# Moving the output transposes and second outputs to other places in the tensor engine's written order

## The chip, the cores and the metric

One NeuronCore of one Trainium2 chip runs the whole program. The metric is the device time of one execution in microseconds (us), lower is better. The kernel before was timed three times: 1958.93, 1961.59 and 1966.63 us, median 1961.59.

## The reference, cut to what matters

One layer of a hybrid encoder is applied to a prompt of 1024 tokens and a sample of 512, both 1024 channels wide: RMSNorm, one projection into eleven blocks of 1024 columns, a bidirectional gated linear recurrence (8 heads of 128) beside a gated short convolution, two branch projections merged by sigmoid gates, an output projection, a residual and a last RMSNorm. What the change touches is the recurrence of one head:

```python
def one_direction(f_raw, lb, reverse):
    logf, one_minus_f = _forget(f_raw, lb)
    ...
    return _gla_chunk_scan(qh, kh, vh, logf)
o = one_direction(f_fw, lb_fw, False) + one_direction(f_bw, lb_bw, True)
o = o * lax.rsqrt(jnp.mean(o * o, axis=-1, keepdims=True) + EPS)
o = o * hnorm_g
...
p_a = jnp.einsum('ble,ed->bld', o_a * jax.nn.silu(z_a), w_a)
# in _gla_chunk_scan, per chunk
o = scores @ v + (q * exp(G)) @ S
S = S * exp(G_last) + k_dec^T @ v
```

## The kernel before, in words

The program has three stages. Up to about 905 us it normalizes the tokens and projects the prompt. From there to about 1519 us a loop runs the recurrence of all heads, with the sample's projections as filling between its small products. After it come the branch and output projections.

The loop makes 25 passes, here called turns (`i`, with `h, m = divmod(i, 3)`); three turns are a round, one for each head `h`. A turn prepares one block of 512 tokens (`cur`) and multiplies the block before it (`prev`). The blocks of a head are the two halves of the prompt (`groups[h]`, blocks 0 and 1) and the sample (`sample[h]`). In turn `m` = 0 `prev` is the sample of the head before, in turn 1 block 0 of this head, in turn 2 block 1.

TensorE (PE) runs in the order in which the source is written (`manual_schedule(engines={T.engine})`); the orders of the other engines and of the queue that issues transfers (SP) are chosen by a planner, which takes earlier written work first among what it holds ready. The pieces of a turn are:

- `near_scores` and `scores` (with `far_scores`): products of 32 and 64 columns (L451, L485), picked into `near` by VectorE (DVE, L464) and copied into `pt` by ScalarE (ACT, L475, L476, L487).
- `transpose_keys` (L500): 6 to 8 transposes of the decayed keys `K` into two PSUM buffers named "u", of which there are three, copied out by ACT (L502).
- `decays`: fourteen ACT copies (L435, L436) and fourteen DVE multiplications (L437, L438) that prepare `K`, `Q` and `cats` of `cur`, and GpSimd (POOL) products `T` (L425).
- `contributions` (L513): what `prev` adds to the states, in two "u" buffers, copied out by ACT (L514). When a group is complete, `states` (DVE, L522) runs the recurrence over chunks.
- `outputs(g, b)` (L537): a block's result in the only "o" buffer; ACT squares it with a sum (L541), DVE and POOL (L542, L81) make the reciprocal root, ACT scales it into `oz` (L545).
- `finish(g)`: four transposes of `oz` for each block in one "u" buffer (L551), a DVE multiplication by the gate `zg` (L552) that frees that buffer, and the store (L553). The prompt's gate `zgp` has one buffer and is loaded on the SP queue.
- `unit()`: one of the sample's projections, 24 products of 512 columns (L77; two of them have 96, L70), here called dense.

The order of PE in a round before, with | around dense units: turn 0: near, keys, outputs of block 0 | unit | scores, contributions | unit | outputs of block 1 | unit. Turn 1: near, keys | unit | scores, contributions | unit | outputs of the sample. Turn 2: near, keys | unit | `finish` of both prompt blocks, scores, `finish` of the sample, contributions | unit, unit. The results that are finished in round `h` are those of head `h - 1`, seven rounds in all; the last head is finished behind the loop.

Of the kernel before, what the change touches and what calls it, by code (L numbers as in the profile page):

```python
# [20 lines left out]
NH = 8  # L21
KT = 8
TB = 512
# [20 lines left out]
def trunk_kernel(ctx: ExitStack, tc: tile.TileContext, xs, w, outs, masks_d, ident_d):  # L44
    nc = tc.nc
    V, A, G, T = nc.vector, nc.scalar, nc.gpsimd, nc.tensor
    load = store = nc.sync.dma_start
# [31 lines left out]
    def rsqrt(pool, t, name):  # L79
        r = pool.tile(list(t.shape), F32, name=f"rs_{name}")  # L80
        G.tensor_tensor(r, t, neghalf[:, :t.shape[-1]], op=ALU.pow)  # L81
        return r
# [25 lines left out]
    zg_d = dram.tile([NH, P, 2 * TB], F32, name="zg_d")  # L108
# [40 lines left out]
    with ExitStack() as st:  # L149
# [178 lines left out]
        for j in range(NH):  # L328
# [7 lines left out]
            for t, pr in enumerate(project2("ff", "fb", j)):  # L336
                for d, z in zip((1, 0), pr):
                    f = cp.tile([P, TB], F32, name="sg", bufs=4)
                    k = cp.tile([P, TB], F32, name="sk", bufs=2)
# [39 lines left out]
    with outer:  # L379
# [7 lines left out]
        def gtile(name, shape, bufs=1):  # L387
            return gp.tile([P, *shape], F32, name=name, bufs=bufs)

        def bank(name, bufs, shape=(CPB, P)):  # L390
            return ps.tile([P, *shape], F32, name=name, bufs=bufs)
# [12 lines left out]
        def loaded(group, b):  # L404

            k = Block(group, b)
            src = fkq_d[k.tb][group.h]
            load(k.F, src[:, 0:2, :])
            load(k.K, src[:, 2:4, :])
            load(k.q, src[:, 4, :])  # L410
            return k

        def decays(k):

            F, K, q = k.F, k.K, k.q
            k.Q = Q = gtile("Q", [2, TB], 3)
            V.scalar_tensor_tensor(Q, ap(q, 0, [[0, 2], [1, TB]]), float(P) ** -0.5, F, op0=ALU.mult, op1=ALU.mult)
            k.kd = gtile("kd", [TB], 2)
            V.tensor_tensor(k.kd, K[:, 0, :], K[:, 1, :], op=ALU.add)

            Ts = [(F, TB)]
            while Ts[-1][1] > CPB:
                t, m = Ts[-1]
                tn = gtile(f"T{TB * 2 // m}", [2, m // 2], 1 if m // 2 > CPB else 4)
                G.tensor_tensor(tn, ap(t, 0, [[m, 2], [2, m // 2]]), ap(t, 1, [[m, 2], [2, m // 2]]), op=ALU.mult)  # L425
                Ts.append((tn, m // 2))
            k.total = Ts[-1][0]
            k.cats = []
            for hs, (t, m) in zip(LEVELS, Ts):
                nb = TB // (2 * hs)  # L430
                cat = gtile("cat", [2, TB], 8)
                k.cats.append(cat)
                kall = ap(K, TB, [[2 * hs, nb], [hs - TB, 2], [1, hs]])
                qall = ap(Q, 0, [[2 * hs, nb], [hs + TB, 2], [1, hs]])
                A.copy(ap(cat, 0, [[2 * hs, nb], [hs, 2], [1, hs]]), kall)  # L435
                A.copy(ap(cat, TB, [[2 * hs, nb], [hs, 2], [1, hs]]), qall)  # L436
                V.tensor_tensor(kall, kall, ap(t, m + 1, [[2, nb], [-m - 1, 2], [0, hs]]), op=ALU.mult)  # L437
                V.tensor_tensor(qall, qall, ap(t, 1, [[2, nb], [m - 1, 2], [0, hs]]), op=ALU.mult)  # L438
# [15 lines left out]
        def near_scores(k):  # L454

            k.sc = []
            score_products(k, range(4))
            k.near = near = gtile("near", [CPB, Q32])
            A.activation(near, k.sc[0][:, 0, :, :], AF.Copy, scale=float(P) ** -0.5)
            for li in range(1, 4):  # L460
                pick(k, li)
# [27 lines left out]
        def chunks_for(k, d):  # L489

            cs = [c for c in range(CPB) if (k.b * CPB + c < k.g.n - 1 if d else k.b * CPB + c > 0)]
            return cs, slice(cs[0], cs[-1] + 1)

        def transpose_keys(k):
            k.kT = []
            for d in (1, 0):
                cs, span = chunks_for(k, d)
                p = bank("u", 3)
                for c in cs:
                    T.transpose(p[:, c, :], k.K[:, d, c * P:(c + 1) * P], ident)  # L500
                kT = gtile("kT", [CPB, P], 2)
                A.copy(kT[:, span, :], p[:, span, :])  # L502
                k.kT.append(kT)

        def contributions(k):
            g = k.g
            if k.b == 0:
                g.us = gtile(f"us{g.n}", [2, g.n, P])
            for d, kT in zip((1, 0), k.kT):
                cs, span = chunks_for(k, d)  # L510
                p = bank("u", 3)
                for c in cs:
                    T.matmul(p[:, c, :], kT[:, c, :], g.v[:, k.b * CPB + c, :], start=True, stop=True)  # L513
                A.copy(g.us[:, d, k.b * CPB + span.start:k.b * CPB + span.stop, :], p[:, span, :])  # L514
            g.done.append(k)
# [9 lines left out]
        def outputs(g, b):  # L525
            for k in g.done[b:b + 1]:
                p = bank("o", 1)
                for c in range(CPB):
                    n = k.b * CPB + c
                    cols = slice(c * P, (c + 1) * P)  # L530
                    mms = [(k.pt[:, c, :], g.v[:, n, :])]
                    if n > 0:
                        mms.append((k.Q[:, 1, cols], g.us[:, 1, n - 1, :]))
                    if n < g.n - 1:
                        mms.append((k.Q[:, 0, cols], g.us[:, 0, n + 1, :]))
                    for m, (l, r) in enumerate(mms):
                        T.matmul(p[:, c, :], l, r, start=m == 0, stop=m == len(mms) - 1)  # L537
                k.oz = oz = gtile("oz", [CPB, P], 3)
                ss = gtile("sso", [CPB], 2)
                for c in range(CPB):  # L540
                    A.activation(oz[:, c, :], p[:, c, :], AF.Square, accum_out=ss[:, c:c + 1])  # L541
                V.tensor_scalar(ss, ss, 1.0 / P, EPS, op0=ALU.mult, op1=ALU.add)  # L542
                r = rsqrt(gp, ss, "o")
                for c in range(CPB):
                    A.activation(oz[:, c, :], p[:, c, :], AF.Copy, scale=r[:, c:c + 1])  # L545

        def finish(g):
            for k in g.done:
                p = bank("u", 3)
                for c in range(CPB):  # L550
                    T.transpose(p[:, c, :], k.oz[:, c, :], ident)  # L551
                V.tensor_tensor(k.oz, p, g.zg[:, k.b * TB:(k.b + 1) * TB].rearrange("p (c t) -> p c t", c=CPB), op=ALU.mult)  # L552
                store(oz_d[k.tb][g.h], k.oz.rearrange("p c t -> p (c t)"))  # L553
# [13 lines left out]
        sample = {}  # L567
# [74 lines left out]
        def prepare(n):  # L642
            while todo and len(ready) < n:
                p, m = todo.pop(0)
                ready.append((m, p()))

        def unit():
            prepare(AHEAD + 1)
            if ready:
                m, x = ready.pop(0)  # L650
                m(x)

        def prompt_group(h):
            return Group(h, (0, 1))
# [7 lines left out]
        groups = [prompt_group(h) for h in range(NH)]  # L662
# [6 lines left out]
        prev = None  # L669
        for i in range(len(order) + 1):  # L670
            h, m = divmod(i, 3)
            cur = None
            if i < len(order):
                cur = nxt if order[i][0] else sample[h]
                if i + 1 < len(order) and order[i + 1][0]:
                    nxt = loaded(*order[i + 1])
            if prev:
                near_scores(prev)
                transpose_keys(prev)
            if m == 0 and h:  # L680
                outputs(groups[h - 1], 0)
            if cur:
                decays(cur)
                if cur.b == 0:
                    values(cur.g)
            unit()
            if m == 2 and h:
                finish(groups[h - 1])
            if prev:
                scores(prev)  # L690
            if m == 2:
                if h:
                    finish(sample[h - 1].g)
                groups[h].zg = gtile("zgp", [2 * TB])
                load(groups[h].zg, zg_d[h])
            if prev:
                contributions(prev)
            unit()
            if m == 0 and h:
                outputs(groups[h - 1], 1)  # L700
            if m == 1 and h:
                outputs(sample[h - 1].g, 0)
            if m != 1:
                unit()
            if prev and len(prev.g.done) == len(prev.g.tbs):
                states(prev.g)
            prev = cur
        outputs(sample[NH - 1].g, 0)
        unit()
        finish(groups[NH - 1])  # L710
        finish(sample[NH - 1].g)
        left.close()
        right.close()

# [328 lines left out]
```

## Time and profile before

| | before |
|---|---|
| median of three runs | 1961.59 us |
| the profiled execution's own time | 1959.61 us |
| its span, first to last instruction | 1957.8 us |
| PE busy | 1918.9 us, 98% of the span |
| DVE busy | 1462.7 us, 75% |
| ACT busy | 941.5 us, 48% |
| mean granted clock of PE | 0.993 |

The profile is of one execution. Its own time is 1.8 us more than its span, and 2.0 us under the median. [...] A timeline row gives the start, the duration, engine, line, operation, out<-in, shape and count, and in brackets the idle time of the engine before it and who ended that. Matmuls are pipelined, so that rows overlap: the time that a piece takes is read from its start to the start of the next piece. All times are from the first instruction.

### The profile page before, as it was taken

The page shows a single profiled execution, that of the slowest core. Times are in us where ns is not written, and L with a number is a line of the kernel's source. Part 1 is how long each engine was busy: PE and PEld are TensorE (multiplying, and loading weights), DVE is VectorE, ACT ScalarE, POOL GpSimd, SP SyncE. Part 2 cuts the span into 40 slices and gives each one's busy share as a digit, 9 for nine tenths or more (in the row PEclk, how much of TensorE's full clock was granted, in tenths as well). Part 3 has the DMA queues.
Part 4 walks back from the last instruction along what each step waited for, and adds up shares of the span by engine and source line. Part 5 has one row for each costly group of instructions (what it writes and reads, how often), then busy time and mean ns, then how long its engine had stood idle before and what let it go on. Part 6 is the DMA issues. An engine that isn't in the chain of part 4 may idle for free.

```text
span 1957.8 us, 38000 instructions
## 1 busy us (share of the span) xinstructions
PE 1918.9 (98%) x14772; PEld 1619.0 (83%) x14772; DVE 1462.7 (75%) x2423; ACT 941.5 (48%) x1946; POOL 144.4 (7%) x220
## 2 busy tenths in 40 slices
PE   8999999999999999999989999999999999999998
PEld 8988888888888888887878888888888888888786
DVE  6558787878787878785776577777773547889996
ACT  6433434434444343434676576676674333434432
POOL 1000000000000000002221122121220000000000
PEclk8999999999999999999999999999999999999999
DMA  7466676676676767668755554554534866879852
GB/s 211 125 212 233 231 232 235 228 238 226 227 245 217 241 230 242 230 211 318 254 184 193 205 196 167 203 198 162 207 132 172 321 232 208 278 236 303 295 175 76
DMA packets 306436, 427.35 MB, mean 218 GB/s; under 512 B 26192, under 2 KB 178000, under 8 KB 306256
## 3 DMA queue, kind: packets, MB, share of 16 engines
q1 hardware_dynamic: 306256, 424.93, 63.9%
q8 instruction: 116, 1.90, 0.4%
q14 instruction: 64, 0.52, 0.1%
HBM read 254.98 MB, written 169.87 MB: 217 GB/s over the span
## 4 chain that ended last, share of the span: by engine, by line
PE 79%; DVE 7%; DMA 4%; issue 4%; ACT 4%; POOL 1%; SPq 0%; DVEq 0%; POOLq 0%; ACTq 0%
PE pp L308 39%; PE pp L77 17%; PE pw L829 9%; PE pp L201 5%; PE pw L77 2%; DVE Q L438 2%; PE o L537 2%; PE u L513 2%; PE sc L451 1%; ACT cat L436 1%; DMA w_raw<-in_w_a 1%; PE pp L70 1%; DVE K L437 1%; POOL rs_o L81 1%; PE u L500 1%
## 5 line engine op out<-in xcount | busy, mean ns | idle before, releaser
L308 PE MATMUL pp<-s_h,w_h 128*128 128x512 f32 x1120 | 435.9, 389 | 1.2 <-ACT w_h L63 1.2
L308 PE MATMUL pp<-s_l,w_h 128*128 128x512 f32 x1120 | 435.7, 389 | 0.0
L308 PE MATMUL pp<-s_h,w_l 128*128 128x512 f32 x1120 | 435.7, 389 | 0.0
L77 PE MATMUL pp<-s_h,w_h 128*128 128x512 f32 x632 | 252.7, 400 | 1.4 <-DMA v<-v_d 0.8
L63 ACT ACTIVATE w_h<-w_raw 128x512 fp32r<-128x512 f32 (+1 forms) x204 | 141.2, 693 | 230.2 <-PE pp L308 151.8
L308 PEld LDWEIGHTS pp<-s_h,w_h 128*128 128x128 f32 x1120 | 210.2, 188 | 45.4 <-ACT w_h L63 1.9
L77 PE MATMUL pp<-s_h,w_l 128*128 128x512 f32 x632 | 247.4, 391 | 0.0
L77 PE MATMUL pp<-s_l,w_h 128*128 128x512 f32 x632 | 246.8, 391 | 0.0
L308 PEld LDWEIGHTS pp<-s_h,w_l 128*128 128x128 f32 x1120 | 210.2, 188 | 43.6
L308 PEld LDWEIGHTS pp<-s_l,w_h 128*128 128x128 f32 x1120 | 210.2, 188 | 43.6
L313 DVE TENSOR_TENSOR tmp<-pp,tmp 128x512 f32<-128x512 f32 x240 | 165.4, 689 | 104.1 <-PE pp L308 103.1
L63 ACT ACTIVATE w_h<-w_S 128x512 fp32r<-128x512 f32 x160 | 99.2, 628 | 186.8 <-PE pp L308 79.6
L64 DVE TENSOR_TENSOR w_l<-w_raw,w_h 128x512 fp32r<-128x512 f32 (+1 forms) x204 | 155.8, 765 | 37.4 <-ACT w_h L63 37.1
L829 PE MATMUL pw<-s_h,w_l 128*128 128x512 f32 x392 | 152.7, 390 | 2.0 <-DVE w_l L64 2.0
L829 PE MATMUL pw<-s_h,w_h 128*128 128x512 f32 x392 | 152.7, 390 | 1.6 <-ACT w_h L63 1.6
L829 PE MATMUL pw<-s_l,w_h 128*128 128x512 f32 x392 | 152.5, 389 | 0.0
L435 ACT COPY cat<-K 128x512 f32<-128x512 f32 x168 | 112.0, 670 | 61.1 <-DVE K L437 23.7
L77 PEld LDWEIGHTS pp<-s_h,w_l 128*128 128x128 f32 x632 | 119.0, 188 | 25.8
L77 PEld LDWEIGHTS pp<-s_h,w_h 128*128 128x128 f32 x632 | 119.5, 189 | 25.0 <-ACT K L132 1.1
L77 PEld LDWEIGHTS pp<-s_l,w_h 128*128 128x128 f32 x632 | 119.6, 189 | 23.4
L436 ACT COPY cat<-Q 128x512 f32<-128x512 f32 x168 | 112.4, 669 | 47.4 <-DVE Q L438 38.3
L438 DVE TENSOR_TENSOR Q<-Q,T 128x512 f32<-128x512 f32 x144 | 111.1, 772 | 27.1 <-ACT cat L436 25.3
(187 smaller groups left out, 3297.9 us busy)
## 6 DMA issues: line engine op xcount, KB each, us to landing
w_raw<-in_w_in SPq DMA_DIRECT2D x80, 512.0 KB, 5.3
ws_d<-w_h SPq DMA_DIRECT2D x160, 256.0 KB, 2.5
ws_d<-w_l SPq DMA_DIRECT2D x160, 256.0 KB, 2.5
w_h<-ws_d SPq DMA_DIRECT2D x79, 512.0 KB, 3.4
w_l<-ws_d SPq DMA_DIRECT2D x79, 512.0 KB, 5.4
fkq_d<-sg SPq DMA_DIRECT2D x48, 256.0 KB, 2.3
v_raw<-in_w_in SPq DMA_DIRECT2D x32, 256.0 KB, 3.5
fkq_d<-sk SPq DMA_DIRECT2D x32, 256.0 KB, 2.3
```

Of the source, the lines that this page charges most:

```text
L63: A.activation(hi, src, AF.Copy)
L64: V.tensor_tensor(lo, src, hi.bitcast(F32), op=ALU.subtract)
L77: T.matmul(out, whl[a][:, k, :], rhs(k, b), start=k == 0 and n == 0, stop=k == KT - 1 and n == 2)
L201: T.matmul(pp, B[f"B{k // 4 + 1}{t + 1}"][a][:, k % 4, c * P:(c + 1) * P], parts[k][b], start=k == 0 and m == 0, stop=k == KT - 1 and m == 2)
L308: T.matmul(bank, hl[x][:, k, :], B[b][y][:, k, :], start=k == 0 and i == 0, stop=k == 3 and i == 2)
L313: V.tensor_tensor(out, p, t, op=ALU.add)
L435: A.copy(ap(cat, 0, [[2 * hs, nb], [hs, 2], [1, hs]]), kall)
L436: A.copy(ap(cat, TB, [[2 * hs, nb], [hs, 2], [1, hs]]), qall)
L438: V.tensor_tensor(qall, qall, ap(t, 1, [[2, nb], [m - 1, 2], [0, hs]]), op=ALU.mult)
L513: T.matmul(p[:, c, :], kT[:, c, :], g.v[:, k.b * CPB + c, :], start=True, stop=True)
L537: T.matmul(p[:, c, :], l, r, start=m == 0, stop=m == len(mms) - 1)
L829: T.matmul(bank, hl[x][:, c:c + P], O[n][y][:, k, :], start=k == 0 and i == 0, stop=k == 3 and i == 2)
```

## The change

`finish` takes a block's number and finishes that block alone. Each turn now finishes one block, right behind its key transposes: turn 0 the sample of the head before the last, turn 1 block 0 and turn 2 block 1 of the last head. The outputs of block 1 (turn 0) and of the sample (turn 1) move up past one dense unit, to stand directly behind the contributions. The load of `zgp` moves from the middle of turn 2 to its start. So each turn has two stretches of small products: one at its start, one between its dense units. What is computed and how many instructions there are stay the same.

```diff
-        def finish(g):
-            for k in g.done:
+        def finish(g, b):
+            for k in g.done[b:b + 1]:
                 p = bank("u", 3)
                 for c in range(CPB):
                     T.transpose(p[:, c, :], k.oz[:, c, :], ident)
@@
                 near_scores(prev)
                 transpose_keys(prev)
+            if i > 3:
+                finish(*((sample[h - 2].g, 0) if m == 0 else (groups[h - 1], m - 1)))
             if m == 0 and h:
                 outputs(groups[h - 1], 0)
+            if m == 2:
+                groups[h].zg = gtile("zgp", [2 * TB])
+                load(groups[h].zg, zg_d[h])
             if cur:
                 decays(cur)
                 if cur.b == 0:
                     values(cur.g)
             unit()
-            if m == 2 and h:
-                finish(groups[h - 1])
             if prev:
                 scores(prev)
-            if m == 2:
-                if h:
-                    finish(sample[h - 1].g)
-                groups[h].zg = gtile("zgp", [2 * TB])
-                load(groups[h].zg, zg_d[h])
-            if prev:
                 contributions(prev)
+            if m < 2 and h:
+                outputs(*((sample[h - 1].g, 0) if m else (groups[h - 1], 1)))
             unit()
-            if m == 0 and h:
-                outputs(groups[h - 1], 1)
-            if m == 1 and h:
-                outputs(sample[h - 1].g, 0)
             if m != 1:
                 unit()
@@
         outputs(sample[NH - 1].g, 0)
         unit()
-        finish(groups[NH - 1])
-        finish(sample[NH - 1].g)
+        for b in range(2):
+            finish(groups[NH - 1], b)
+        finish(sample[NH - 1].g, 0)
```

## Rows read from the trace of the kernel before

**Rows 1.** The page: busy time of each engine, share of the span, instructions.
```profile
PE 1918.9 (98%) x14772; PEld 1619.0 (83%) x14772; DVE 1462.7 (75%) x2423; ACT 941.5 (48%) x1946; POOL 144.4 (7%) x220
```

**Rows 2.** The page: the chain that ended last, shares by engine.
```profile
PE 79%; DVE 7%; DMA 4%; issue 4%; ACT 4%; POOL 1%; SPq 0%; DVEq 0%; POOLq 0%; ACTq 0%
```

**Rows 3.** Waits of PE, whole span: us in total, times, longest.
```profile
PE u L513 <- DVE oz L552: 13.9, 7, 2.4
...
PE u L513 <- ACT us L514: 2.5, 1, 2.5
PE pw L829 <- DVE w_l L64: 2.0, 3, 0.8
```

**Rows 4.** Timeline of PE, turn 2 of heads 3 (first row) and 4.
```profile
1185.42 3.19 PE L513 MATMUL u<-v,kT 128*128 128x128 f32 x14 [2.27 <-DVE oz L552]
...
1246.08 0.98 PE L500 MATMUL u<-ident,K 128*128 128x128 f32 x7
1246.82 0.48 PE L77 MATMUL pp<-s_h,w_h 128*128 128x512 f32 x1
...
1252.38 1.03 PE L551 MATMUL u<-ident,oz 128*128 128x128 f32 x8
...
1254.94 0.66 PE L551 MATMUL u<-ident,oz 128*128 128x128 f32 x4
1257.79 1.83 PE L513 MATMUL u<-v,kT 128*128 128x128 f32 x14 [2.19 <-DVE oz L552]
1259.38 0.48 PE L77 MATMUL pp<-s_h,w_h 128*128 128x512 f32 x1
```

**Rows 5.** Windows over the three falls of the granted clock (PEclk) in the loop.
```profile
1024.46:1031.28 6.82, 5.95 (x18) 5.08 (x19) 6.82 (x16) 5.29 (x14) 2.03 (x4) 0.50 0.37 88
1184.88:1188.30 3.42, 2.88 (x13) 2.88 (x14) 3.42 (x8) 2.31 (x6) 0.69 (x2) 0.50 0.65 192
1399.92:1403.34 3.42, 3.42 (x15) 3.39 (x16) 3.07 (x7) 2.28 (x6) 0.29 (x1) 0.50 0.77 238
```

**Rows 6.** Timeline of DVE, turns 1 and 2 of head 4.
```profile
1240.31 0.73 DVE L437 TENSOR_TENSOR K<-K,T 128x512 f32<-128x512 f32 x1
...
1257.06 1.28 DVE L552 TENSOR_TENSOR oz<-u,zgp 128x512 f32<-128x512 f32 x2
...
1267.14 1.48 DVE L522 SCALAR_TENSOR_TENSOR us<-us,T 128x128 f32<-128x128 f32 x4
```

**Rows 7.** Timeline of PE, turn 0 of head 4.
```profile
1211.05 1.60 PE L513 MATMUL u<-v,kT 128*128 128x128 f32 x12
1217.98 0.38 PE L537 MATMUL o<-v,pt 128*128 128x128 f32 x2
```

**Rows 8.** Timeline of PE, turn 0 of head 5.
```profile
1272.47 0.39 PE L537 MATMUL o<-v,pt 128*128 128x128 f32 x2
...
1274.85 0.47 PE L77 MATMUL pp<-s_h,w_h 128*128 128x512 f32 x1
```

**Rows 9.** Timeline of ACT, head 4.
```profile
1207.00 1.15 ACT L545 ACTIVATE oz<-o,rs_o 128x128 f32<-128x128 f32 x4 [0.30 <-POOL rs_o L81]
...
1242.36 0.48 ACT L514 COPY us<-u 128x384 f32<-128x384 f32 x1
...
1244.91 0.28 ACT L541 ACTIVATE oz<-o 128x128 f32<-128x128 f32 x1 [0.70 <-PE o L537]
...
1248.15 1.14 ACT L545 ACTIVATE oz<-o,rs_o 128x128 f32<-128x128 f32 x4 [1.50 <-POOL rs_o L81]
...
1271.31 0.69 ACT L435 COPY cat<-K 128x512 f32<-128x512 f32 x1 [5.21 <-PE sc L451]
```

**Rows 10.** Waits of ACT, whole span.
```profile
ACT oz L545 <- POOL rs_o L81: 21.2, 24, 1.7
```

**Rows 11.** Timeline of POOL, turn 1 of head 4.
```profile
1235.79 1.42 POOL L425 TENSOR_TENSOR T<-F 128x512 f32<-128x512 f32 x1 [12.61 <-DVE F L134]
```

**Rows 12.** Timeline of the SP queue, turn 2 of head 4.
```profile
1258.77 2.17 SPq L695 DMA_DIRECT2D zgp<-zg_d  x1
```

## The prediction

> **What bounds the kernel now.** I read the busy times first. TensorE is busy for 98% of the span, DVE for 75%, ACT for 48% [rows 1], and 79% of the chain that ended last runs on TensorE [rows 2]: this kernel's time is TensorE's work plus its pauses. So the waits of TensorE come next. One stands far above the rest: `contributions` (L513) waits for the DVE multiplication of L552, 13.9 us in 7 waits, and once more 2.5 us for ACT's copy of L514. Behind the loop nothing larger than the 2.0 us of L829 is listed, so time won in the loop isn't lost to a wait that is already known there [rows 3].
>
> Seven waits are one for each round in which a head is finished, and the timeline of one of them shows why. Turn 2 sends eight transposes of `finish` at 1252.38 us, four more at 1254.94, and then wants a "u" buffer for the contributions. There are three. The first finish buffer comes free when DVE has multiplied it, and TensorE goes on only at 1257.79, after 2.19 us of idle time [rows 4]. By the pace of the key transposes (seven from 1246.08 to 1246.82, 0.106 us each) the first eight were through at about 1253.2; DVE started that multiplication at 1257.06 and took 0.64 us for each of the two [rows 6]: it was at the `decays` of the next block, which stand earlier in the source.
>
> [...]
>
> **The change part by part.** *Finish.* No instruction is added or removed: twelve transposes, three multiplications and three stores in each round are spread over three turns. A turn now takes five "u" buffers (two for keys, one for the finish, two for contributions), where turn 2 took seven. The contributions come one dense unit and the score products after the finish: from 1246.82 to 1252.38 for the unit and 1.7 us for the scores (1253.2 to 1254.94), 7.3 us in all [rows 4]. DVE needs 0.64 us within it, and as `finish` is now written ahead of `decays`, it should come early. What it gives:
>
> - the listed waits: 13.9 + 2.5 = 16.4 us [rows 3];
> - the half clock: TensorE was busy 5.95 + 2.88 + 3.42 = 12.25 us in the three stretches [rows 5]. At full clock the same work takes half: 6.1 us;
> - the restart: four transposes began at 1254.94 and the contributions at 1257.79, 2.85 us, of which 2.19 are listed as idle. Four transposes take 0.42 at the pace above. That leaves 0.24 us, of which I take 0.2 in each of seven: 1.4 us [rows 4].
>
> Sum 23.9 us. From below this part is worth 0, if the same lateness turns up elsewhere; from above no more than these 23.9, since there are no other pauses of this kind.
>
> *Second outputs.* Block 1's outputs moved from 1217.98 to behind the contributions that start at 1211.05 [rows 7], the sample's likewise in turn 1. The products stay (2.38 us for one block, 1272.47 to 1274.85 [rows 8]). TensorE alternates once less between small and dense in a round. No row shows a pause at such a change by itself; bounded by the restart of 0.24 us, the largest step in these rows, eight rounds are 2 us, and turn 2 may lose as much, since a unit is now followed there by score products and no longer by transposes. I count 0, with 2 us on both sides. The "o" buffer must be free for the outputs earlier: ACT scaled the first block from 1207.00 to 1208.15 [rows 9], and twelve contributions at 0.114 us (1.59 for fourteen [rows 4]) ended at about 1212.4, so 4 us remain. What gets easier: `Q`, `v` and the states' buffer are released one unit (5.6 us) earlier to DVE and to the transfers.
>
> *Stores and the gate's load.* The three stores go out one in each turn. The `zgp` load waits for the multiplication of block 1, and on the SP queue it now stands ahead of turn 2's other loads. Before, it held the queue for 2.17 us at 1258.77 [rows 12]. What would stand behind it are the next units' weights, which the code asks for three units ahead, 3 x 5.6 = 16.7 us before their use [rows 4]. A hold of 2 or 3 us is hidden. Cost 0; uncovered it would be at most the same 2.17 us in each of eight rounds, 17 us, and I see no path for it.
>
> *What is late next.* TensorE comes to the next turn 3.4 us earlier (23.9 / 7). Its inputs there: the states of the head end at 1268.62 [rows 6] and its outputs use them at 1272.47 [rows 8], 3.85 us of room; the finish that now stands ahead adds 0.4 us, and DVE has two multiplications (1.28 us) less in front of the states. Room left: 3.85 + 0.4 + 1.28 - 3.4 = 2.1 us. The last `K` of block 1 ended at 1241.04, 5.0 us ahead of the transposes at 1246.08 [rows 4, 6]. ACT, at 1271.31, waited 5.21 us for TensorE's score products to release a `cat` buffer [rows 9]: the chain of copies and multiplications through ACT and DVE runs ahead of TensorE by more than the 3.4 us that it loses.
>
> The sum: 1959.6 - 23.9 = 1935.7 us against the profiled execution's own time. That execution lay 2.0 us under the median of the three runs, by which it would be 1937.7. I forecast **1937 us**.
>
> **The rivals.** *A smaller wait at the new place.* In turn 2 the finish needs the third "u" buffer 0.7 us after the key transposes start, and it is the last one that ACT copied out in turn 1, at 1242.36 to 1242.84. It is needed at 1246.82: 4.0 us of room [rows 4, 9]. The sample's outputs now put their ACT work ahead of that point: from the first square at 1244.91 to the end of the scaling at 1249.29 it took 4.4 us, 0.7 of it a `cat` copy and 1.5 a wait for POOL [rows 9]. If all 3.7 us go in front of the copy, with a DVE multiplication of 0.7, TensorE waits 0.4 us; if POOL's product of 1.42 us [rows 11] also stands in front of the root, 1.8 us. Over seven rounds that is 3 to 13 us given back: 1940 to 1950. For it speaks that ACT already waited for POOL in 24 of 24 outputs, 0.9 us each [rows 10]; against it, that the copy is written ahead of the outputs and may go first. [...]
>
> *The gain is given back.* If the chain through DVE and ACT, not the buffers, sets the round's 71 us, TensorE waits for states or `K` what it waits for L552 now: about 1959. The 5.21 us for which ACT waited for TensorE [rows 9] speak against it; it would have to be under 3.4.
>
> *Slower: the clock.* Turn 0's second stretch grows to scores 1.7, contributions 1.6 and outputs 2.4, 5.7 us of small products in a row, in eight rounds. If such a stretch by itself brought the clock down for 6.82 us, as the first of the three falls did [rows 5], it would cost 3.4 us each, 27 us in all, and the time would be 1963; it decides from 3.0 us for each (23.9 / 8). Against it: the stretch of turn 2 from 1252.38 to 1259.38 was 7.0 us of small products with 2.19 us of idle time in it, and four of seven such stretches kept the full clock [rows 4, 5]. [...]
>
> **How the numbers follow.** The forecast, all seven pauses gone and nothing new above 1 us: 0.72, with 1932 to 1941 as its own range (2 us between median and profiled execution, 2 us of alternation, and the rest for waits under 1 us). The smaller wait, 1940 to 1950: 0.17. Given back, about 1959: 0.06. Slower by the clock, or half of it: 0.05. The range to 1949 leaves out the last two and the tail of the second, to 1932 a little below: 1932 to 1949. A measurement of this kernel can tell about 0.5%, 9.8 us, from no change: faster is under 1951.8, slower over 1971.4. The forecast and nearly all of the second case lie under it, and half of the clock rival: 0.88 faster. The given back gain and most of the rest: 0.08 the same. Slower, by the clock or by a wait of several us in each turn: 0.04.
>
> **What would show it.** Right: the wait of L513 for L552 is gone from TensorE's list, a round takes 67 to 68 us from near scores to near scores instead of 71, the half clock no longer appears in the loop, and DVE's L552 comes three times in a round, one shortly after each turn's key transposes. The part on the outputs is right if no wait of L537 appears. Wrong: a wait of L551 or L500 for ACT's L514 in turn 2 (the first rival), of L537 for L522 or of L500 for L437 (the second), or windows at 0.50 behind turn 0's contributions (the third). The planner's order for ACT and DVE, which no row of before shows, is what would most easily make the forecast wrong.

## The result, and the profile after

The changed kernel takes 1935.68 us (median of four runs, 1934.11 to 1938.16) against 1960.26 us before (four runs, 1958.39 to 1966.63). The ratio is 0.987, with a 95% interval from 0.9844 to 0.9896: 1.3% faster. The profiled execution lasted 1938.16 us by its own time and 1936.4 by its span.

On the page after, the busy times: DVE, ACT and TensorE do the same work as in [rows 1], and TensorE's share is 99%.

```profile
PE 1911.7 (99%) x14772; PEld 1612.7 (83%) x14772; DVE 1457.9 (75%) x2423; ACT 941.7 (49%) x1946; POOL 152.8 (8%) x220
```

The chain that ended last, by engine. TensorE has 87% of it, where [rows 2] gave 79; DVE has 5 instead of 7, ACT 1 instead of 4.

```profile
PE 87%; DMA 5%; DVE 5%; issue 1%; ACT 1%; SPq 0%; POOL 0%; DVEq 0%; POOLq 0%; ACTq 0%
```

The longest waits of TensorE after. The two rows of L513 that headed [rows 3], 13.9 and 2.5 us, are not in the list any more, and no wait of L537 or L551 has come in. What is left at the top lies ahead of the loop or behind it, but for L500's 1.4 us, which stand at the loop's start (908.83), as they did before.

```profile
PE tp L163 <- issue: 2.7, 2, 2.1
PE pw L825 <- ACT w_h L63: 2.6, 2, 1.6
PE pw L825 <- DVE w_l L64: 2.6, 3, 1.2
PE pp L77 <- ACT K L132: 2.0, 1, 2.0
PE u L500 <- DVE K L437: 1.4, 1, 1.4
```

The timeline of TensorE after, turn 2 of head 4, which answers to [rows 4].

```profile
1185.75 0.46 PE L451 MATMUL sc<-q,kd 128*32 128x32 f32 x32
...
1231.86 0.46 PE L451 MATMUL sc<-q,kd 128*32 128x32 f32 x32
...
1233.14 0.98 PE L500 MATMUL u<-ident,K 128*128 128x128 f32 x7
1233.96 0.60 PE L551 MATMUL u<-ident,oz 128*128 128x128 f32 x4
1234.31 0.48 PE L77 MATMUL pp<-s_h,w_h 128*128 128x512 f32 x1
...
1239.98 1.06 PE L451 MATMUL sc<-cat 128*32 128x32 f32 x96
1241.58 1.83 PE L513 MATMUL u<-v,kT 128*128 128x128 f32 x14
1243.16 0.48 PE L77 MATMUL pp<-s_h,w_h 128*128 128x512 f32 x1
1254.25 0.46 PE L451 MATMUL sc<-q,kd 128*32 128x32 f32 x32
```

The finish of one block now stands between the keys' transposes and the dense unit, the contributions follow the scores without an idle bracket, and the next unit's first product starts at 1243.16, 1.58 us after theirs. A round, from the near scores of head 4 to those of head 5, takes 1254.25 - 1185.75 = 68.5 us.

The windows over the loop, first near scores to last finish, and over what follows it: the columns are the length, the busy time of PE, PEld, DVE, ACT and POOL with their counts, the granted clock (a share of full speed: the half clock is 0.50), the share of the DMA engines and GB/s. First before, then after.

```profile
905.90:1518.80 612.90, 593.44 (x8542) 506.43 (x8542) 430.28 (x782) 402.89 (x1043) 120.25 (x183) 0.99 0.55 193
1518.80:1957.80 439.00, 427.31 (x1885) 352.17 (x1883) 344.00 (x509) 159.79 (x248) 8.53 (x12) 0.99 0.70 237
```

```profile
906.10:1494.20 588.10, 585.47 (x8542) 499.90 (x8542) 426.19 (x782) 403.25 (x1043) 128.59 (x183) 1.00 0.58 200
1494.20:1936.40 442.20, 428.93 (x1885) 353.31 (x1883) 343.29 (x509) 159.85 (x248) 8.54 (x12) 0.99 0.70 235
```

The same 8542 products of the loop take 24.8 us less. TensorE's busy time in it fell by 8.0 us only; the other 16.8 us were idle time (19.5 before, 2.6 after). Behind the loop this execution took 3.2 us more. Up to half of a stretch at half clock is in that, at a place where before had none (1.00 from 1814.60 to 1818.05):

```profile
1814.62:1818.03 3.41, 3.41 (x10) 2.64 (x9) 3.41 (x6) 2.62 (x4) 0.00 (x0) 0.50 0.81 272
```

Such a stretch stands in some of the other profiles below and not in others (finishes only with four additions has one, with 0.84 in the window from 1809.65 to 1813.06 and 0.66 from there to 1816.47; outputs only has 1.00 in every window behind the loop up to 1929.00), so it isn't put down to the change. The two profiled spans differ by 21.4 us; the medians differ by 24.6, close to what the loop alone gives.

### The profile page after: what moved, and what is told of

Read it like the earlier page. It is cut to its first block, busy times and chain, and to the rows that moved or that the text cites. A ratio compares the mean times of both kernels' runs of the same rounds, so it can differ in the third digit from the quotient of the medians.

```text
span 1936.4 us, 38016 instructions
## 1 busy us (share of the span) xinstructions
PE 1911.7 (99%) x14772; PEld 1612.7 (83%) x14772; DVE 1457.9 (75%) x2423; ACT 941.7 (49%) x1946; POOL 152.8 (8%) x220
## 4 chain that ended last, share of the span: by engine, by line
PE 87%; DMA 5%; DVE 5%; issue 1%; ACT 1%; SPq 0%; POOL 0%; DVEq 0%; POOLq 0%; ACTq 0%
PE pp L308 39%; PE pp L77 21%; PE pw L825 9%; PE pp L201 5%; PE o L537 3%; PE sc L451 3%; PE u L513 2%; PE pp L70 2%; DMA w_raw<-in_w_a 1%; PE u L500 1%; DVE w_l L64 1%; DVE s_l L64 1%; PE sc L485 1%; DMA io<-oz_p 1%; DMA w_l<-wv_d 1%
## 5 line engine op out<-in xcount | busy, mean ns | idle before, releaser
L437 DVE TENSOR_TENSOR K<-K,T 128x512 f32<-128x512 f32 x144 | 108.9, 756 | 22.9 <-ACT cat L435 21.0
```

## The experiments

Each kernel is one edit. Unless the text says that it is made to the kernel before, the edit is made to the changed kernel. The ratio is to the kernel before, run on the same chip; the chip is not the same in all experiments, and the median of the kernel before goes from 1960.26 to 1962.63 us over them.

**Finishes only.** The finishes stand as in the change, the second outputs at their old places behind the unit.

```diff
                 contributions(prev)
-            if m < 2 and h:
-                outputs(*((sample[h - 1].g, 0) if m else (groups[h - 1], 1)))
             unit()
+            if m == 0 and h:
+                outputs(groups[h - 1], 1)
+            if m == 1 and h:
+                outputs(sample[h - 1].g, 0)
```

> The finishes are spread as in the changed kernel; the second outputs stay where they were, behind the next dense unit. Buffer theory (turn 2 asked for seven of three u buffers, two of them given back by late DVE multiplications): all seven pauses of the contributions are gone, no fall of the clock in the loop, 1936 to 1939 us. Late-DVE theory (DVE began turn 2 late because the sample's outputs held Q; moving the outputs is what helps): the pauses stay in good part, 1948 to 1960 us. Alternation theory (fewer stretches of small products): three stretches in turn 0 as before, so at most half of the gain, 1946 us or more.

Measured: 1936.94 us (four runs, 1935.02 to 1937.47), ratio 0.9868 (0.9848 to 0.9889). No wait of L513, and a mean granted clock of 0.996 over the profiled execution (0.993 in the kernel before). The spread finishes alone have the whole gain, with three stretches of small products in turn 0 as before. So one stretch less in a round is worth nothing that these runs can tell. This run can't tell fewer requests for a buffer from more time for DVE: in turn 2 of head 4, L552 ended at 1237.76 and the contributions began at 1240.87.

**Outputs only.** This edit is made to the kernel before: the second outputs move up, the finishes stay in turn 2.

```diff
             if prev:
                 contributions(prev)
+            if m < 2 and h:
+                outputs(*((sample[h - 1].g, 0) if m else (groups[h - 1], 1)))
             unit()
-            if m == 0 and h:
-                outputs(groups[h - 1], 1)
-            if m == 1 and h:
-                outputs(sample[h - 1].g, 0)
```

> Only the second outputs move up; all three finishes stay in turn 2 behind the unit. Buffer theory: the contributions of turn 2 still take the two buffers of the prompt's finishes, so the waits for L552 stay, 10 us or more of the 13.9, and the time is 1952 to 1962 us. Late-DVE theory: DVE gets Q one unit earlier, reaches L552 about 2.5 us earlier and the waits fall under 4 us, 1937 to 1944 us.

Measured: 1936.89 us (four runs, 1936.29 to 1938.74), ratio 0.9872 (0.9851 to 0.9892). This was not expected: the part that I had priced at nothing also has the whole gain by itself. What happened is in turn 2 of head 4, TensorE first and then DVE:

```profile
1230.50 0.46 PE L451 MATMUL sc<-q,kd 128*32 128x32 f32 x32
...
1238.08 1.04 PE L551 MATMUL u<-ident,oz 128*128 128x128 f32 x8
...
1241.54 1.83 PE L513 MATMUL u<-v,kT 128*128 128x128 f32 x14 [0.24 <-DVE oz L552]
```

```profile
1227.31 1.21 DVE L417 SCALAR_TENSOR_TENSOR Q<-q,F 128x1024 f32<-128x1024 f32 x1
...
1240.81 1.28 DVE L552 TENSOR_TENSOR oz<-u,zgp 128x512 f32<-128x512 f32 x2
```

Eight transposes go out at 1238.08 and DVE multiplies at 1240.81, 2.73 us later, not 4.68 as before (1252.38 to 1257.06, [rows 4, 6]). The wait is the same one, shrunk to 0.24 us here; it is the only one of the seven that is listed at all. Why DVE is earlier is read from the rows: the sample's outputs read `Q`. As they are issued one unit earlier, the next `Q` (L417) is written 3.2 us before turn 2's near scores. In the kernel before these two rows stood the other way round, 0.6 us apart; one turn earlier the same instruction is seen waiting for outputs (L537):

```profile
1244.80 0.46 PE L451 MATMUL sc<-q,kd 128*32 128x32 f32 x32
```

```profile
1220.63 1.23 DVE L417 SCALAR_TENSOR_TENSOR Q<-q,F 128x1024 f32<-128x1024 f32 x1 [0.42 <-PE o L537]
...
1245.39 1.19 DVE L417 SCALAR_TENSOR_TENSOR Q<-q,F 128x1024 f32<-128x1024 f32 x1
```

No run frees `Q` alone, by a further buffer for it, so this link is not tested by itself; that DVE's lateness decides here is tested below, with additions.

**One finish per turn, behind the unit.** This edit, too, is made to the kernel before. The outputs stay at their old places, and each finish stands directly ahead of the scores, where no dense unit lies between it and the contributions. `finish(g, b)` is that of the changed kernel.

```diff
             unit()
-            if m == 2 and h:
-                finish(groups[h - 1])
+            if i > 3:
+                finish(*((sample[h - 2].g, 0) if m == 0 else (groups[h - 1], m - 1)))
             if prev:
                 scores(prev)
             if m == 2:
-                if h:
-                    finish(sample[h - 1].g)
```

> One finish in each turn, but behind the first dense unit, directly ahead of the scores, so that the contributions follow it by 1.6 us and not by a unit; outputs at their old places. Buffer theory: the contributions take the two buffers of the key transposes, which ACT has long copied out, so no wait for L552, 1936 to 1942 us. If instead what matters is the unit's time between finish and contributions for DVE, the waits of L513 for L552 stay at 1 us or more in each of 21 turns and the time is 1950 us or more. A new wait of TensorE for K or near scores, because DVE's multiplication is planned ahead of the unit's end and holds DVE's order, would show as L500 or L451 waits and give 1945 to 1960 us.

Measured: 1937.18 us (four runs, 1936.42 to 1939.35), ratio 0.9873 (0.9852 to 0.9894), no wait of L513. In turn 2 of head 4 the contributions start only 2.1 us after the finish, without idle time, and 2.5 us before DVE comes to the finish's multiplication:

```profile
1237.85 0.60 PE L551 MATMUL u<-ident,oz 128*128 128x128 f32 x4
...
1239.98 1.83 PE L513 MATMUL u<-v,kT 128*128 128x128 f32 x14
```

```profile
1242.46 0.68 DVE L552 TENSOR_TENSOR oz<-u,zgp 128x512 f32<-128x512 f32 x1
```

So the contributions don't use the finish's buffer at all. The 7.3 us of distance, on which the prediction leaned, aren't needed: it does to ask for five buffers in a turn and not for seven.

**The sample's finish only.** Again an edit to the kernel before. The finishes of both prompt blocks and the second outputs stay; only the sample's finish leaves turn 2, for turn 0. Turn 2 then asks for six buffers.

```diff
                 transpose_keys(prev)
+            if m == 0 and i > 3:
+                finish(sample[h - 2].g)
             ...
                 scores(prev)
             if m == 2:
-                if h:
-                    finish(sample[h - 1].g)
```

> Only the sample's finish leaves turn 2, for turn 0; the two prompt finishes stay behind turn 2's unit, so turn 2 asks for six u buffers. Buffer theory, with buffers taken in turn: the first contribution takes the buffer of a key transpose, the second that of the first prompt finish, which DVE frees 2 us or more after it is wanted: the wait stays at 8 to 16 us in all and the time at 1948 to 1960 us. A theory in which each finish moved away brings a third: 1951 us with 9 us of waits, and no wait that has moved from the first to the second contribution.

Measured: 1956.65 us (ten runs, 1953.02 to 1959.40), ratio 0.9974 (0.9961 to 0.9986). The waits are back in all seven rounds, 13.6 us, and so are three stretches at half clock:

```profile
PE u L513 <- DVE oz L552: 13.6, 7, 2.6
```

```profile
1020.69:1024.10 3.41, 3.38 (x12) 3.09 (x13) 3.41 (x6) 2.24 (x6) 1.63 (x1) 0.50 0.21 77
1181.12:1184.53 3.41, 3.41 (x10) 2.64 (x9) 2.92 (x7) 3.31 (x9) 0.53 (x2) 0.50 0.91 244
1252.80:1256.21 3.41, 3.41 (x12) 3.12 (x13) 3.41 (x7) 2.27 (x6) 0.29 (x1) 0.50 0.47 160
```

The timeline of turn 2 shows the buffers being counted. With one request less, the first direction's six instructions run, and the second's eight wait for DVE, as they do in all seven rounds:

```profile
1246.74 1.04 PE L551 MATMUL u<-ident,oz 128*128 128x128 f32 x8
...
1249.31 0.94 PE L513 MATMUL u<-v,kT 128*128 128x128 f32 x6
1252.80 2.07 PE L513 MATMUL u<-v,kT 128*128 128x128 f32 x8 [2.56 <-DVE oz L552]
```

The third stretch begins at that pause's end, 1252.80. Against finishes only, on the same chip, this kernel takes 1956.65 - 1936.94 = 19.7 us more: 13.6 are the waits, 10.20 us of work at half clock give 5.1, an estimate that takes half the time for the same work at full clock, and 1.0 is left over. In the second stretch the dense products follow each other at 0.43 us (1181.80 to 1183.93), behind it at 0.23 (1184.67 to 1185.83).

**Two "u" buffers.** The changed kernel with one buffer less, in all three places that ask for one.

```diff
-                p = bank("u", 3)
+                p = bank("u", 2)
```

> The changed kernel with two u buffers and not three: the finish now needs a key transpose's buffer back from ACT's copy L502, which ended 1.6 to 2.9 us behind the finish's place in turns 1 and 2 of head 4. Buffer theory: TensorE waits at L551 in each of 21 turns for 1 to 3 us, 30 to 60 us in all, with the clock falling to 0.50 behind some of them; 1965 to 2010 us. If the third buffer is not needed, 1936 to 1945 us.

Measured: 1985.52 us, one run. The finish waits for ACT's copy of the keys in all 21 places:

```profile
PE u L551 <- ACT kT L502: 36.4, 21, 3.7
```

So even with the requests spread evenly the third buffer is needed: without it TensorE waits 36.4 us, the mean granted clock is 0.991 (0.995 in the changed kernel), and the kernel is slower than before. Behind a pause of 2.77 us that ended at 1016.56 the dense products follow each other at 0.43 us (1017.95 to 1019.66), and from 1020.48 on at 0.23.

**A late DVE, four additions.** To test how much lateness each part alone stands, DVE gets spare additions after the sample's `Q` (their results are unused). One was put into outputs only, one into finishes only, one into the changed kernel.

```diff
             V.scalar_tensor_tensor(Q, ...)
+            if k.g.n == CPB:
+                for _ in range(4):
+                    V.tensor_tensor(gtile("spare", [TB]), Q[:, 0, :], Q[:, 1, :], op=ALU.add)
```

Outputs only:

> The kernel with only the second outputs moved, and four additional DVE additions of 0.7 us (results unused) behind the sample's Q, so that DVE comes about 2.8 us later to turn 2's work. If moving the outputs cured the wait only by bringing DVE there just in time (its longest wait was 0.2 us), the waits of L513 for L552 come back, 10 us or more, and the time is 1948 to 1960 us. If there is slack for another reason, it stays at 1936 to 1939 us.

Measured: 1937.76 us (four runs, 1935.84 to 1940.85), ratio 0.9879 (0.9865 to 0.9894). Four waits of L513 (L516 in this kernel) for DVE came, but of 1.6 us together, not the 10 that were expected: most of the added 2.7 us (4 x 0.68) went into gaps in which DVE had waited anyway. In turn 2 of head 4 its multiplication came 3.03 us after the transposes (1239.41 to 1242.44), only 0.3 us later than without them. A test too weak to decide.

Finishes only:

> The kernel with only the finishes spread, and the same four additions. Buffer theory: no contribution needs a buffer that DVE frees, so 2.8 us more of lateness cost nothing: no wait of L513, 1935 to 1940 us. If the spread, too, was only a matter of DVE being just in time, waits of L513 or of L500 for K appear and the time is 1945 us or more.

Measured: 1942.12 us (four runs, 1939.27 to 1945.26), ratio 0.9905 (0.9889 to 0.9922), slower than the 1935 to 1940 expected. The "u" buffers held: there is no wait of L513. But the outputs (L540 here) waited for DVE:

```profile
PE o L540 <- DVE cu L617: 2.7, 3, 1.1
```

The row names the instruction that ended last, a memset of the sample's convolution. The product that waits reads the states `us`, though, and their last step (L525 here) ended at 1257.45, just before the product went on at 1257.50:

```profile
1257.11 0.34 DVE L525 SCALAR_TENSOR_TENSOR us<-us,T 128x128 f32<-128x128 f32 x1
```

```profile
1257.50 0.49 PE L540 MATMUL o<-us,Q 128*128 128x128 f32 x2 [1.09 <-DVE cu L617]
```

So it is the states that come late here. The profiled execution is the fastest of the four (1939.27); where the rest of the median's rise went isn't settled.

The changed kernel:

> The changed kernel with the same four additions: as the one before, no wait of L513, 1935 to 1940 us by the buffer theory; 1945 us or more if DVE's place in turn 2 is what decides.

Measured: 1936.24 us (four runs, 1935.32 to 1939.01), ratio 0.9872 (0.9858 to 0.9887), no new wait. On the same chip that is 5.9 us less than finishes only with the same additions: with a late DVE the outputs' earlier place is worth something. The states end at 1251.04 here, 2.9 us before the outputs begin at 1253.92.

**Eight additions.** The same in outputs only and in the changed kernel, with `range(8)`.

> Only the second outputs moved, with eight additions instead of four behind the sample's Q, about 2.4 us more of DVE work ahead of turn 2's multiplications; with four, L552's waits were 1.6 us in 4. If moving the outputs works by bringing DVE there in time, the waits of the contributions for the finish multiplication are now 8 to 20 us in all and the time is 1945 to 1960 us; if it stays under 3 us of such waits, lateness of DVE is not what that version hangs on.

Measured: 1955.38 us (five runs, 1953.66 to 1958.12), ratio 0.996 (0.9945 to 0.9975). The old wait is back at its old size (L516 and L555 are L513 and L552 here), and three stretches of 3.41 us at half clock with it:

```profile
PE u L516 <- DVE oz L555: 13.3, 8, 2.5
```

```profile
1177.37:1180.78 3.41, 3.33 (x15) 3.31 (x16) 3.33 (x8) 2.83 (x7) 0.88 (x3) 0.50 0.75 185
1020.36:1023.77 3.41, 3.01 (x15) 3.01 (x15) 3.41 (x7) 1.78 (x5) 0.66 (x1) 0.50 0.52 173
1392.41:1395.82 3.41, 3.33 (x15) 3.31 (x16) 3.33 (x8) 2.83 (x7) 0.88 (x3) 0.50 0.73 178
```

> The changed kernel with eight additions. Buffer theory: still no wait of a contribution for the finish multiplication; the states of the head had 2.8 us of room with four additions, so at most small waits of the outputs for them, 1935 to 1942 us. If DVE's place decides, the same waits as in the version with only the outputs moved.

Measured: 1937.77 us (four runs, 1934.85 to 1942.44), ratio 0.9881 (0.9864 to 0.9898). The changed kernel takes some 5 us more of DVE work in each round (8 x 0.68 = 5.4), and its median lies 2.1 us over that without them, less than its runs' scatter; the kernel before, on this chip, lies 2.4 us higher too. The first sign of the next limit is there, the outputs waiting for the states:

```profile
PE o L540 <- DVE us L525: 1.4, 4, 0.4
```

No kernel of these beats the changed one by more than the scatter: finishes only, outputs only, one finish behind the unit and the changed kernel lie within 1.5 us of each other, with ratios from 0.9868 to 0.9873.

## Why the prediction was right, and where its working was not

**The time, and the sum.** 1937 was forecast and 1935.68 measured; the sum was 23.9 us, and the loop gave 24.8. Its terms hold. The seven waits and the one for L514 are gone (16.4 us), and the loop's idle time fell by 16.8. The half clock is gone from the loop: 6.1 us were expected, an estimate by which the same work takes half the time at full clock. In the first stretch before, the dense products follow each other at 0.427 us (1028.06 to 1030.62), behind it at 0.230 (1031.63 to 1033.93), a factor of 1.86. TensorE's busy time in the loop fell by 593.44 - 585.47 = 8.0, in which more than the half clock may lie. The round of head 4 shrank by 2.5 us (71.0 to 68.5), which is its own wait of 2.19 and 0.3 more; I had named 67 to 68, from spreading all 23.9 us evenly over seven rounds, though the half clock sits in three of them, and not in this one. One of the eight waits is not explained by the count of requests: in head 1 the second contribution went on at 1025.33, when ACT had copied out the first (L514), and before DVE began the second multiplication (1027.22). Which buffer it took the trace doesn't show.

**What the gain was put down to.** Here a step failed. "Second outputs ... I count 0" is the right price beside the spread finishes, since finishes only and the changed kernel are equal. But it was read as a part without effect, with what it makes easier mentioned and not pursued. Outputs only shows that it would have brought the whole gain alone. The wait has two conditions, and both must hold: turn 2 must ask for so many "u" buffers that a contribution needs one which DVE frees, and DVE must come late to L552. The change removes the first, and it moves the next `Q` as outputs only does (to 1228.69, 3.2 us before the near scores at 1231.86). The gain isn't the sum of its parts, 24 + 0, but either one's.

How late is too late can be read off. From the start of the eight transposes to the start of L552 it took 4.68 us before, with a wait of 2.19; 4.30 in outputs only with eight additions (1244.57 to 1248.87), with 1.81; and 2.73 us in outputs only, with 0.24. Each time the difference is 2.49 us. So the point lies at about 2.5 us, and outputs only stands on the edge of it. That is what the two parts together buy: with eight additions outputs only falls back to 1955.38, while the changed kernel stays at 1937.77; with four, finishes only takes 1942.12 and the changed kernel 1936.24.

**"DVE's L552 comes shortly after each turn's key transposes": not in turn 2.** The finish is written ahead of `decays`, but DVE does not do it ahead of them:

```profile
1238.24 0.68 DVE L552 TENSOR_TENSOR oz<-u,zgp 128x512 f32<-128x512 f32 x1
```

The transposes went out at 1233.96, 4.3 us earlier, almost as far back as in the kernel before; in turn 1 it is 1.5 us and in turn 0 3.0. It costs nothing because by the source nobody needs that buffer before the next turn. The 7.3 us of distance, as said, were not the reason either; the number of requests is, as one finish behind the unit (contributions that run before L552) and the sample's finish only (waits with six requests) show from both sides.

**The first rival, a smaller wait in turn 2: it did not come.** ACT copies the third buffer out ahead of the outputs' squares, not behind them:

```profile
1229.48 0.48 ACT L514 COPY us<-u 128x384 f32<-128x384 f32 x1
1229.86 0.28 ACT L541 ACTIVATE oz<-o 128x128 f32<-128x128 f32 x1
...
1232.49 1.15 ACT L545 ACTIVATE oz<-o,rs_o 128x128 f32<-128x128 f32 x4 [0.61 <-POOL rs_o L81]
```

From 1229.96 to the finish at 1233.96 there are 4.0 us of room, what it was before. Had the copy stood behind the scaling, it would have come at 1233.64 to 1234.12, and TensorE would have waited 0.2 us. Two "u" buffers show what a finish that waits for an ACT copy costs, there that of the keys (L502): 36.4 us in 21 waits.

**Given back: no, with little to spare.** I worked out 2.1 us of room for the states. In the changed kernel they end at 1253.73 and the outputs begin at 1256.68, 2.95 us:

```profile
1253.39 0.34 DVE L522 SCALAR_TENSOR_TENSOR us<-us,T 128x128 f32<-128x128 f32 x1
```

```profile
1256.68 0.39 PE L537 MATMUL o<-v,pt 128*128 128x128 f32 x2
```

Four additions bring no wait, eight bring 1.4 us in four rounds; how much of them reaches the states was not read.

**Slower by the clock: no.** Turn 0's second stretch came as foreseen, 5.4 us of small products without a pause, from 1196.21 to the unit behind the outputs at 1201.62, and the window over it reads:

```profile
1195.00:1203.00 8.00, 8.00 (x158) 7.20 (x157) 5.74 (x10) 6.13 (x14) 2.66 (x4) 1.00 0.36 134
```

The clock is 1.00 there, with TensorE busy for 8.00 of 8.00 us, and none of the eight such stretches fell: over the whole loop, 906.10 to 1494.20, the clock is 1.00. The falls shown for the kernel before, the sample's finish only and outputs only with eight additions are nine; each begins within a pause of 1.80 to 2.51 us or at most 1.32 us behind the end of one of 1.99 to 2.56 us.

**The gate's load: nothing.** It held the SP queue for 2.17 us before [rows 12] and 0.42 now:

```profile
1239.35 0.42 SPq L686 DMA_DIRECT2D zgp<-zg_d  x1
```

## What to carry to other kernels

A wait on a buffer that a late engine frees can have two causes at once, as here: too many requests in one stretch and too late a consumer. Look for the cheapest way to break either, and break both if you want margin. Before pricing an edit at nothing, ask what it releases earlier and who is first in that engine's queue: here output products that moved up by one unit came with a next `Q` 3.8 us earlier against TensorE's near scores, with L552 1.95 us earlier against its transposes, and with 0.2 us left of 13.9 us of waits. Count the requests for a buffer in order of issue in each stretch: with seven or six requests for three buffers a contribution needed one that DVE frees, with five it did not.

## What was not expected of the hardware

Seven or eight pauses of up to 2.6 us in a loop of some 610 us cost more than they last. Waits of 13.3, 13.6 and 16.4 us came each time with three stretches at a granted clock of 0.50, of 3.41 or 6.82 us, and the whole was worth 17.6 us (outputs only with eight additions, against the changed kernel with the same), 19.7 (the sample's finish only, against finishes only) and 24.6 (the kernel before, against the changed one). Each of these nine stretches begins within a pause or at most 1.32 us behind its end, as in outputs only with eight additions:

```profile
1392.49 3.45 PE L516 MATMUL u<-v,kT 128*128 128x128 f32 x14 [1.80 <-DVE oz L555]
```

From 1392.41 on, just within this pause of 1.80 us, the clock is at 0.50; behind the longer one of 2.19 us that ended at 1257.79 in the kernel before [rows 4] it is at 1.00 (1257.79 to 1261.20). With two "u" buffers, behind a pause of 2.72 us the four transposes take 1.11 us, behind one of 2.71 us 0.66:

```profile
1181.30 1.11 PE L551 MATMUL u<-ident,oz 128*128 128x128 f32 x4 [2.72 <-ACT kT L502]
...
1257.37 0.66 PE L551 MATMUL u<-ident,oz 128*128 128x128 f32 x4 [2.71 <-ACT kT L502]
```

So a pause's length alone doesn't select the ones that fall, and what does stays open.
